# A streamed fp32 encoder layer: where the row work of 32 gathered tokens stands in VectorE's queue, and an expert product with both activation parts in one matmul

## The chip, the cores and the metric

The kernel runs on one core of a Trainium2 chip. The metric is the device time of one execution in microseconds. Engines are named as in the profile: PE (TensorE matmul), PEld (its weight load), DVE (VectorE), ACT (ScalarE), POOL (GpSimd) and SP (SyncE, which here only starts transfers).

## The reference, cut to what matters

One layer over 256 tokens of width 2048 in fp32. The work in question is its last part, a feed-forward layer of 16384 experts of one neuron each, of which each token uses 8 heads times 16:

```python
def block(args):
    xb, eb, gb = args          # tokens, their expert numbers, their gates
    u = expert_u[eb]
    pre = jnp.einsum('bd,bed->be', xb, u)
    act = gelu(pre) * gb
    return jnp.einsum('be,bed->bd', act, expert_v[eb])
```

`expert_u` and `expert_v` are 16384 x 2048 each, 128 MB, and are read from HBM.

## The kernel before, in words

**Two ways through the experts.** The first 224 tokens (`T`) are computed dense: every expert's first product for every token, times a gate that is zero for unused experts, and then every expert's second product. The last 32 tokens (`SP`) take the expert rows that they need: 32 times, POOL starts an indirect DMA (L766) that brings one row of 2048 values to each of the 128 partitions into one of three row buffers, and DVE reduces it against the tokens (L789, which ends in a short readout of the sum); then 32 times a row of `peer_v` that DVE scales and adds up (L802, L804). These 64 instructions are called the rows here.

**The weight stream.** All large operands come as tiles `w` of 128 x 2048 (1 MB) in `wtile`: SP starts the transfer into one of three buffers, ACT casts the tile to a rounded `wh` (L95), DVE subtracts to the rest `wl` (L97); `wh` and `wl` have two buffers each. With `pool=512` POOL does the last 512 of the 2048 columns of `wl` (L99 and L100). The activations are split in the same way, and a product is three products: high by high, low by high, high by low.

**The stages.** `u_steps(q)` for q = 0..3 does the first product, 32 tiles each: per tile 16 pairs of a matmul of 448 columns (`wh` with the high and low half of the tokens side by side, L834) and one of 224 (`wl`, L835), then ACT copies one half of the result (L837), DVE adds the other (L838), ACT applies GELU (L839); the results are the tiles `P0` to `P7` of 16 each. During `u(1)` the steps of `gate_steps` make the dense gates: DVE builds one-hots (L860, L862), PE multiplies them (L877), POOL writes them to `gd` in HBM. `prep_steps(c)` loads the gates of one `P` in two transfers of 0.9 MB into buffers of the same ring as the weights (L910), multiplies (16 instructions, L913) and splits into `ah` and `al` (L104 on ACT, L105 on DVE). `v_steps(q)` does the second product, 32 tiles each: for two values of n, four output blocks `ds` of four tiles `e`; per tile 16 triples of 224 columns (L956 to L958) into four PSUM banks, one for each f. After the fourth tile of a block, DVE adds each bank to `yT` (L964; for n = 0 ACT copies it, L962). The banks come from a pool of four, so a block's bank is the next block's.

**What sets the order.** `run_spread` and `with_last` set in which order the program is written: the rows are spread over the steps of `v(0)`, `u(2)`, `v(1)`, `u(3)`, `v(2)`, `v(3)`, the gate steps over `u(1)`, and `prep` over the last steps of the `u` stages and steps within `v`. A scheduler then places each engine's instructions by readiness on a clock of its own, and each engine runs its list in that order. The context `tc.issue_after(i)` keeps an instruction behind the instruction `i` in that placing. Before, none of the rows has such an edge.

Of the kernel before, what the change touches and what calls it, by code (L numbers as in the profile page):

```python
# [34 lines left out]
def block_kernel(ctx: ExitStack, tc: tile.TileContext, a: dict, out: bass.AP):  # L35
# [735 lines left out]
    def sparse_input():  # L771
        two = [X([P, 2, D], F32, f"rows{i}") for i in range(2)]
        bufs.extend((two[0][:, 1], two[1][:, 0], two[1][:, 1]))
        xs = two[0][:, 0]
# [8 lines left out]
        nc.vector.scalar_tensor_tensor(xs, xs, rs, gb, op0=ALU.mult, op1=ALU.mult)  # L783
        return xs

    def sparse_steps(xs):
# [11 lines left out]
        for k in range(SP):  # L798
            g = rows_of(a["peer_v"], k)
            ak = act[:, k : k + 1]  # L800
            if k == 0:
                nc.vector.tensor_scalar(y, g, ak, None, op0=ALU.mult)  # L802
            else:
                nc.vector.scalar_tensor_tensor(y, g, ak, y, op0=ALU.mult, op1=ALU.add)  # L804
# [96 lines left out]
    def prep_steps(c):  # L901
# [13 lines left out]
        for e in range(4):
            ah = M([P, 4, T], F32R, f"ah{c}_{e}")
            pv = pt[:, 4 * e : 4 * e + 4, :]
            al = M([P, 4, T], F32R, f"al{c}_{e}")
            split(ah, al, pv)
            parts[c, e] = (ah, al)  # L920
            yield
# [157 lines left out]
```

## Time and profile before

| | |
|---|---|
| median of 3 runs | 2864.82 us (2861.01 to 2867.58) |
| the profiled execution | 2864.39 us |
| its span in the trace | 2862.6 us |
| mean granted clock of PE | 0.945 of full speed |
| `u(0)` to the end (from 1094.4 us) | 1768.2 us |

| stage | from | to | us | tiles |
|---|---|---|---|---|
| `u(0)`, `u(1)` | 1094.4 | 1596.4 | 502.0 | 64 |
| `v(0)` | 1596.4 | 1940.4 | 344.0 | 32 |
| `u(2)` | 1940.4 | 2111.0 | 170.6 | 32 |
| `v(1)` | 2111.0 | 2291.7 | 180.7 | 32 |
| `u(3)` | 2291.7 | 2462.2 | 170.5 | 32 |
| `v(2)`, `v(3)` | 2462.2 | 2849.5 | 387.3 | 64 |
| the rest | 2849.5 | 2862.6 | 13.1 | |

The stages are cut at PE's first matmul of each, and tiles are counted from 0 over `u(0)` and `u(1)` (0 to 63), `v(0)` (64 to 95) and so on. A time of this table is where one tile's matmuls begin.

### The profile page before, as it was taken

Reading aid. Unit: us, or ns where it says so; the run is one execution under the profiler, and the core shown is the slowest. Engines: PE = TensorE matmul, PEld = TensorE weight load, DVE = VectorE, ACT = ScalarE, POOL = GpSimd, SP = SyncE. Lnnn points to the kernel's source line nnn. Section 1 sums busy time; section 2 is a strip of 40 time slices with the busy share of each in tenths; the row PEclk is TensorE's granted clock in tenths of the full one; section 3 lists DMA queues with packets and bytes.
Section 4 is the critical chain, followed back from the end, with each engine's and each line's share of the span. In section 5 each row is a group of like instructions: output and inputs, shape, how many; then the busy total and the mean of one; then the engine's idle time right before and its main releaser. Section 6 shows DMA issues by size and latency. Waiting matters only on the chain. (4 is left out here: it accounts for less than half of the span.)

```text
span 2862.6 us, 38540 instructions
## 1 busy us (share of the span) xinstructions
PE 2546.0 (89%) x16314; PEld 2330.4 (81%) x16314; DVE 1648.3 (58%) x1961; ACT 1154.2 (40%) x1314; POOL 305.7 (11%) x216
## 2 busy tenths in 40 slices
PE   8999999999999998696688733499999999999998
PEld 7888888888888887695688633499989998899898
DVE  5655444565554579944776656745555455455554
ACT  5444334454444454342354301134443344333343
POOL 0000000000000001263344225300000000000000
PEclk9999999999999999898799866699999999999999
DMA  6544556545444644375676677755555555755553
GB/s 251 197 171 177 191 191 220 191 177 182 172 165 175 209 174 148 111 254 217 235 230 225 250 273 293 279 203 208 204 205 219 202 206 190 284 190 190 196 184 133
DMA packets 84812, 584.65 MB, mean 204 GB/s; under 512 B 9792, under 2 KB 9856, under 8 KB 18720
## 3 DMA queue, kind: packets, MB, share of 16 engines
q1 hardware_dynamic: 67904, 480.28, 47.2%
q0 software_dynamic: 16592, 101.88, 9.9%
q8 instruction: 128, 2.10, 0.3%
q14 instruction: 44, 0.36, 0.0%
q10 hardware_dynamic: 144, 0.03, 0.0%
HBM read 559.58 MB, written 22.54 MB: 203 GB/s over the span
## 5 line engine op out<-in xcount | busy, mean ns | idle before, releaser
L97 DVE TENSOR_TENSOR wl<-w,wh 128x2048 fp32r<-128x2048 f32 (+2 forms) x400 | 862.6, 2163 | 770.2 <-ACT wh L95 770.0
L95 ACT CAST wh<-w 128x2048 fp32r<-128x2048 f32 (+2 forms) x464 | 841.2, 1818 | 893.8 <-PE v L957 403.5
L958 PE MATMUL v<-ah,wl 128*128 128x224 f32 x2048 | 582.8, 285 | 145.6 <-DVE wl L97 145.6
L834 PE MATMUL u<-a,wh 128*128 128x448 f32 x2048 | 679.8, 388 | 3.4 <-ACT wh L95 3.4
L835 PE MATMUL u<-a,wl 128*128 128x224 f32 x2048 | 558.8, 273 | 74.2 <-DVE wl L100 60.9
L956 PE MATMUL v<-ah,wh 128*128 128x224 f32 x2048 | 582.3, 284 | 24.0 <-ACT yT L962 14.1
L957 PE MATMUL v<-al,wh 128*128 128x224 f32 x2048 | 577.9, 282 | 0.0
L958 PEld LDWEIGHTS v<-ah,wl 128*128 128x128 f32 x2048 | 411.7, 201 | 149.1 <-DVE wl L97 149.1
L835 PEld LDWEIGHTS u<-a,wl 128*128 128x128 f32 x2048 | 408.0, 199 | 81.0 <-DVE wl L100 65.9
L956 PEld LDWEIGHTS v<-ah,wh 128*128 128x128 f32 x2048 | 411.9, 201 | 26.5 <-ACT yT L962 14.5
L834 PEld LDWEIGHTS u<-a,wh 128*128 128x128 f32 x2048 | 401.6, 196 | 35.5 <-ACT wh L95 3.9
L957 PEld LDWEIGHTS v<-al,wh 128*128 128x128 f32 x2048 | 411.3, 201 | 0.5 <-issue 0.5
L839 ACT ACTIVATE P<-P 128x224 f32<-128x224 f32 x128 | 50.1, 391 | 371.0 <-DVE P L838 371.0
L100 POOL TENSOR_TENSOR wl<-w,wh 128x512 fp32r<-128x512 f32 x64 | 138.2, 2160 | 291.2 <-ACT wh L95 225.8
L100 DVE TENSOR_TENSOR wl<-w,wh 128x1536 fp32r<-128x1536 f32 x64 | 114.5, 1790 | 94.6 <-ACT wh L95 94.6
L119 PE MATMUL g<-wh,x 128*128 128x512 f32 x256 | 100.2, 391 | 0.0
L121 PE MATMUL g<-wl,x 128*128 128x512 f32 x256 | 99.6, 389 | 0.0
L120 PE MATMUL g<-wh,x 128*128 128x512 f32 x256 | 99.6, 389 | 0.0
L141 PE MATMUL mq<-hq,wh 128*128 128x512 f32 x256 | 90.8, 399 | 0.0
L141 PE MATMUL pq<-hf,wh 128*128 128x512 f32 x256 | 90.8, 398 | 0.0
L141 PE MATMUL qk<-x,wh 128*128 128x512 f32 x256 | 90.2, 397 | 0.2 <-DVE qk L147 0.2
L141 PE MATMUL mk<-mem,wh 128*128 128x512 f32 x256 | 89.7, 396 | 0.0
(323 smaller groups left out, 3554.9 us busy)
## 6 DMA issues: line engine op xcount, KB each, us to landing
w<-in_peer_uT SPq DMA_DIRECT2D x128, 1024.0 KB, 4.8
w<-in_peer_vP SPq DMA_DIRECT2D x128, 1024.0 KB, 4.8
w<-in_w_in SPq DMA_DIRECT2D x72, 1024.0 KB, 4.8
w<-in_mem_w_kv SPq DMA_DIRECT2D x32, 1024.0 KB, 4.8
w<-in_w_out SPq DMA_DIRECT2D x16, 1024.0 KB, 4.8
w<-in_mem_w_q SPq DMA_DIRECT2D x16, 1024.0 KB, 4.8
w<-in_mem_w_o SPq DMA_DIRECT2D x16, 1024.0 KB, 4.9
w<-in_peer_w_q SPq DMA_DIRECT2D x16, 1024.0 KB, 4.8
```

Source lines behind the costliest of these rows:

```text
L95: nc.scalar.copy(wh[:, c], w[:, c])
L97: nc.vector.tensor_tensor(wl[:, c], w[:, c], wh[:, c].bitcast(F32), op=ALU.subtract)
L100: e.tensor_tensor(wl[:, c], w[:, c], wh[:, c].bitcast(F32), op=ALU.subtract)
L119: nc.tensor.matmul(po[b], xh, wh[:, k, :], start=(kk == 0), stop=False)
L120: nc.tensor.matmul(po[b], xl, wh[:, k, :], start=False, stop=False)
L121: nc.tensor.matmul(po[b], xh, wl[:, k, :], start=False, stop=(kk == nkc * 4 - 1))
L141: nc.tensor.matmul(po[f], wh[:, k, fs], xT.both(kk), start=(kk == 0), stop=False)
L834: nc.tensor.matmul(po[:, 0 : 2 * T], wh[:, k, :], aT.both(k), start=(k == 0), stop=False)
L835: nc.tensor.matmul(po[:, 0:T], wl[:, k, :], aT.tiles[k // 8][:, k % 8, 0], start=False, stop=(k == NK - 1))
L956: nc.tensor.matmul(o, wh[:, j, fs], ah[:, j, :], start=first, stop=False)
L957: nc.tensor.matmul(o, wh[:, j, fs], al[:, j, :], start=False, stop=False)
L958: nc.tensor.matmul(o, wl[:, j, fs], ah[:, j, :], start=False, stop=last)
```

## The change

1. `wtile` notes the last DVE instruction that makes a `wl`. Each row instruction, the product that makes the tokens' input (L783) and the gate products of `prep` are written with `issue_after` that instruction, so that they stand behind the `wl` of the latest tile written.
2. `sparse_input` takes a row buffer for `g_ffn` instead of a weight buffer, and its product is written after `u(1)` instead of before it.
3. `u(1)` no longer gives 512 columns to POOL; the gate steps are spread over 25 tiles instead of 27.
4. `prep`: transfer and products are a step apart, both halves of an activation part stand in one tile `ahl` of two experts' width (8 tiles instead of 4 pairs), and `prep(2)` becomes the first part of the spread stages. It gets 7 last steps of a `u` stage instead of 6. The rows are spread over 174 steps instead of 168.
5. `v_steps`: 16 pairs of 448 and 224 columns per tile in place of 16 triples of 224. The bank's two halves are added to `yT` by two DVE instructions; for n = 0 ACT copies one and DVE adds the other.

```diff
@@ wtile
-                nc.vector.tensor_tensor(wl[:, c], w[:, c], wh[:, c].bitcast(F32), op=ALU.subtract)
+                last_split[0] = nc.vector.tensor_tensor(wl[:, c], w[:, c], wh[:, c].bitcast(F32), op=ALU.subtract).ins
...
@@ sparse_input
-        xs = two[0][:, 0]
+        xs, gb = two[0][:, 0], bufs[2]
...
-        n_w[0] += 1
-        gb = stream.tile([P, D], F32, tag="w", name=f"w{n_w[0]}", bufs=3)
...
-        nc.vector.scalar_tensor_tensor(xs, xs, rs, gb, op0=ALU.mult, op1=ALU.mult)
-        return xs
+        yield
+        with tc.issue_after(last_split[0]):
+            nc.vector.scalar_tensor_tensor(xs, xs, rs, gb, op0=ALU.mult, op1=ALU.mult)
+        yield xs
@@ sparse_steps (the rows of peer_v likewise)
-            nc.vector.tensor_tensor_reduce(
-                g, g, xs, 1.0, 0.0, op0=ALU.mult, op1=ALU.add, accum_out=act[:, k : k + 1]
-            )
+            with tc.issue_after(last_split[0]):
+                nc.vector.tensor_tensor_reduce(
+                    g, g, xs, 1.0, 0.0, op0=ALU.mult, op1=ALU.add, accum_out=act[:, k : k + 1]
+                )
@@ u_steps
-            wh, wl = wtile(a["peer_uT"][j], 512 if q < 2 else 0)
+            wh, wl = wtile(a["peer_uT"][j], 512 if q == 0 else 0)
@@ prep_steps
-        for b in range(2):
-            n_w[0] += 1
-            g = stream.tile([P, T // 16, 8, 16], F32, tag="w", name=f"w{n_w[0]}", bufs=3)
-            nc.sync.dma_start(g, gd[:, 2 * c + b])
-            for j in range(8):
-                pv = pt[:, 8 * b + j, :].rearrange("p (b t) -> p b t", t=16)
-                nc.vector.tensor_tensor(pv, pv, g[:, :, j, :], op=ALU.mult)
+        g = []
+        for b in range(3):
+            if b > 0:
+                with tc.issue_after(last_split[0]):
+                    for j in range(8):
+                        pv = pt[:, 8 * b - 8 + j, :].rearrange("p (b t) -> p b t", t=16)
+                        nc.vector.tensor_tensor(pv, pv, g[b - 1][:, :, j, :], op=ALU.mult)
+            if b < 2:
+                n_w[0] += 1
+                g.append(stream.tile([P, T // 16, 8, 16], F32, tag="w", name=f"w{n_w[0]}", bufs=3))
+                nc.sync.dma_start(g[b], gd[:, 2 * c + b])
             yield
...
+            for i in range(2):
+                ahl = M([P, 2, 2, T], F32R, f"a{c}_{e}{i}")
+                j = 4 * e + 2 * i
+                split(ahl[:, :, 0, :], ahl[:, :, 1, :], pt[:, j : j + 2, :])
+                parts[c, 2 * e + i] = ahl
@@ v_steps
-                            nc.tensor.matmul(o, wh[:, j, fs], ah[:, j, :], start=first, stop=False)
-                            nc.tensor.matmul(o, wh[:, j, fs], al[:, j, :], start=False, stop=False)
-                            nc.tensor.matmul(o, wl[:, j, fs], ah[:, j, :], start=False, stop=last)
+                            ahl = parts[c, 2 * e + j // 2][:, j % 2]
+                            nc.tensor.matmul(
+                                po[f][:, 0 : 2 * T], wh[:, j, fs], ahl.rearrange("p e t -> p (e t)"),
+                                start=first, stop=False,
+                            )
+                            nc.tensor.matmul(po[f][:, 0:T], wl[:, j, fs], ahl[:, 0, :], start=False, stop=last)
...
-                                nc.scalar.copy(y, o)
+                                nc.scalar.copy(y, po[f][:, T : 2 * T])
                             else:
-                                nc.vector.tensor_tensor(y, y, o, op=ALU.add)
-                    if ds == 3 or (ds, e) in ((1, 0), (2, 0)):
+                                nc.vector.tensor_tensor(y, po[f][:, T : 2 * T], y, op=ALU.add)
+                            nc.vector.tensor_tensor(y, po[f][:, 0:T], y, op=ALU.add)
+                    if ds == 3 or (ds, e) in ((1, 0), (1, 3), (2, 2)):
...
@@ the stages
-    xs = sparse_input()
-    run_spread(u_steps(1), 27, gate_steps(), T // TB + 1)
-    run(prep_steps(2))
+    sp = sparse_input()
+    next(sp)
+    run_spread(u_steps(1), 25, gate_steps(), T // TB + 1)
+    xs = next(sp)
     rest = chain(
+        prep_steps(2),
         v_steps(0),
-        with_last(u_steps(2), 6, prep_steps(4)),
+        with_last(u_steps(2), 7, prep_steps(4)),
...
-    run_spread(rest, 168, sparse_steps(xs), 2 * SP + 1)
+    run_spread(rest, 174, sparse_steps(xs), 2 * SP + 1)
```

Three places show what moves. All are lists of DVE, and a line number of the changed kernel is a few higher than that of the same line before (L789 is L794, L97 is L98, L804 is L810, L913 is L919). A row of L789 is two instructions, the second being the readout.

**Place 1, DVE early in `v(0)`.** `wl256` and `wl258` are the rest parts of two weight tiles, `rows` the row buffers. Before:

```order
L97 TENSOR_TENSOR wl256_12163<-w256_12160,wh256_12162 128x2048
L789 ISA rows1_9662,act_8013<-rows1_9662,rows0_9661 128x2048
L789 ISA act_8013 128x1
L789 ISA rows1_9662,act_8013<-rows1_9662,rows0_9661 128x2048
L789 ISA act_8013 128x1
L789 ISA rows1_9662,act_8013<-rows1_9662,rows0_9661 128x2048
L789 ISA act_8013 128x1
L97 TENSOR_TENSOR wl258_12227<-w258_12224,wh258_12226 128x2048
L789 ISA rows1_9662,act_8013<-rows1_9662,rows0_9661 128x2048
L789 ISA act_8013 128x1
L789 ISA rows1_9662,act_8013<-rows1_9662,rows0_9661 128x2048
L789 ISA act_8013 128x1
```

The change, in the same stage:

```order
L98 TENSOR_TENSOR wl253_11994<-w253_11991,wh253_11993 128x2048
L98 TENSOR_TENSOR wl254_12032<-w254_12029,wh254_12031 128x2048
L794 ISA rows0_9661,act_8013<-rows0_9661 128x2048
L794 ISA act_8013 128x1
L98 TENSOR_TENSOR wl255_12084<-w255_12081,wh255_12083 128x2048
L976 TENSOR_TENSOR yT_11908<-v2_0_0_11909,yT_11908 128x224
L976 TENSOR_TENSOR yT_11908<-v2_0_1_11910,yT_11908 128x224
L976 TENSOR_TENSOR yT_11908<-v2_0_2_11911,yT_11908 128x224
L98 TENSOR_TENSOR wl257_12124<-w257_12121,wh257_12123 128x2048
L976 TENSOR_TENSOR yT_11908<-v2_0_3_11912,yT_11908 128x224
L98 TENSOR_TENSOR wl258_12162<-w258_12159,wh258_12161 128x2048
L794 ISA rows1_9662,act_8013<-rows1_9662,rows0_9661 128x2048
```

Before, three rows stand between `wl256` and `wl258` and five between `wl258` and `wl259`; in the change at most one row stands between two `wl`.

**Place 2, DVE at the border of `u(1)` and `v(0)`.** `u62` and `u63` are the last results of `u(1)`, `P3` their tile, and `w257` the gates of half a `prep`. Before:

```order
L97 TENSOR_TENSOR wl252_11937<-w252_11934,wh252_11936 128x2048
L838 TENSOR_TENSOR P3_10850<-u62_11807,P3_10850 128x224
L97 TENSOR_TENSOR wl253_11991<-w253_11988,wh253_11990 128x2048
L838 TENSOR_TENSOR P3_10850<-u63_11850,P3_10850 128x224
L97 TENSOR_TENSOR wl254_12045<-w254_12042,wh254_12044 128x2048
L913 TENSOR_TENSOR P3_10850<-P3_10850,w257_12214 128x224 x8
L97 TENSOR_TENSOR wl255_12101<-w255_12098,wh255_12100 128x2048
L97 TENSOR_TENSOR wl256_12163<-w256_12160,wh256_12162 128x2048
```

The change (`w249` and `w250` are the gates of `prep(2)`, `a2_00` and so on the parts that the first tile of `v(0)` and those after it use, `wl248` belongs to the last tile of `u(1)`, and `wl251` to the first of `v(0)`; five more `a2` parts and one more row follow before `wl251`):

```order
L844 TENSOR_TENSOR P3_10862<-u60_11691,P3_10862 128x224
L98 TENSOR_TENSOR wl248_11821<-w248_11818,wh248_11820 128x2048
L844 TENSOR_TENSOR P3_10862<-u61_11733,P3_10862 128x224
L787 SCALAR_TENSOR_TENSOR rows0_9661<-rows0_9661,rs_9663,rows1_9662 128x2048
L919 TENSOR_TENSOR P2_9673<-P2_9673,w249_11860 128x224 x8
L919 TENSOR_TENSOR P2_9673<-P2_9673,w250_11870 128x224 x8
L794 ISA rows0_9661,act_8013<-rows0_9661 128x2048
L794 ISA act_8013 128x1
L844 TENSOR_TENSOR P3_10862<-u62_11775,P3_10862 128x224
L108 TENSOR_TENSOR a2_00_11882<-P2_9673,a2_00_11882 128x2x224
L108 TENSOR_TENSOR a2_01_11885<-P2_9673,a2_01_11885 128x2x224
L108 TENSOR_TENSOR a2_10_11888<-P2_9673,a2_10_11888 128x2x224
```

All 16 products of `prep(2)`, the tokens' product L787, two rows and the eight parts stand between the last `wl` of `u(1)` and the first of `v(0)`; before, that `prep` stands between the `wl` of three tiles of `u(1)`, and here there is one `P` addition or one group of eight products (those of `prep(3)`) between two `wl`.

**Place 3, DVE where one output block of `v` ends and the next begins** (`v4_0_0` is the bank f = 0 of block 0 of c = 4). Before:

```order
L97 TENSOR_TENSOR wl324_15429<-w324_15426,wh324_15428 128x2048
L964 TENSOR_TENSOR yT_11929<-yT_11929,v4_0_0_15194 128x224
L964 TENSOR_TENSOR yT_11929<-yT_11929,v4_0_1_15195 128x224
L964 TENSOR_TENSOR yT_11929<-yT_11929,v4_0_2_15196 128x224
L964 TENSOR_TENSOR yT_11929<-yT_11929,v4_0_3_15197 128x224
L97 TENSOR_TENSOR wl326_15493<-w326_15490,wh326_15492 128x2048
L97 TENSOR_TENSOR wl327_15549<-w327_15546,wh327_15548 128x2048
```

The change, at such a place with a row:

```order
L98 TENSOR_TENSOR wl341_15596<-w341_15593,wh341_15595 128x2048
L975 TENSOR_TENSOR yT_11908<-v5_0_0_15423,yT_11908 128x224
L810 SCALAR_TENSOR_TENSOR rows0_9661<-rows1_9662,act_8013,rows0_9661 128x2048
L976 TENSOR_TENSOR yT_11908<-v5_0_0_15423,yT_11908 128x224
L975 TENSOR_TENSOR yT_11908<-v5_0_1_15424,yT_11908 128x224
L975 TENSOR_TENSOR yT_11908<-v5_0_2_15425,yT_11908 128x224
L976 TENSOR_TENSOR yT_11908<-v5_0_1_15424,yT_11908 128x224
L976 TENSOR_TENSOR yT_11908<-v5_0_2_15425,yT_11908 128x224
L975 TENSOR_TENSOR yT_11908<-v5_0_3_15426,yT_11908 128x224
L976 TENSOR_TENSOR yT_11908<-v5_0_3_15426,yT_11908 128x224
L98 TENSOR_TENSOR wl342_15636<-w342_15633,wh342_15635 128x2048
```

The four additions behind a `wl` became eight, and at some blocks a row stands between the two additions of one bank. Of the 28 blocks with n above 0, seven have a row among their additions.

## Rows read from the trace of the kernel before

**Rows 1.** The page: its first line and PE's part of the 40 slices of 71.6 us each (busy share and granted clock in tenths).
```profile
span 2862.6 us, 38540 instructions
...
PE   8999999999999998696688733499999999999998
...
PEclk9999999999999999898799866699999999999999
```

**Rows 2.** Busy time by stretch: the stretch, its length, then busy us and count of PE, PEld, DVE, ACT and POOL, the granted clock, the DMA share and GB/s. The stretches are tiles 30 and 31 of `u`, `u(1)`, the 20 tiles of `u(1)` from tile 40 on, `v(0)`, a part of `v(0)`, `u(2)`, `v(1)`, `u(3)` and `v(2)` with `v(3)`.
```profile
1297.90:1322.80 24.90, 15.15 (x70) 13.71 (x68) 10.89 (x9) 4.85 (x6) 6.11 (x3) 0.73 0.56 210
1322.80:1596.40 273.60, 208.71 (x1474) 191.96 (x1473) 191.42 (x220) 116.65 (x213) 109.64 (x72) 0.90 0.67 227
1421.00:1565.00 144.00, 127.27 (x980) 117.27 (x978) 110.33 (x124) 74.84 (x148) 65.95 (x42) 0.98 0.68 225
1596.40:1940.40 344.00, 201.95 (x1538) 199.02 (x1537) 208.37 (x146) 69.99 (x58) 88.39 (x50) 0.77 0.70 261
1629.00:1849.00 220.00, 81.20 (x476) 78.82 (x477) 145.99 (x95) 23.33 (x24) 84.70 (x48) 0.64 0.75 284
1940.40:2111.00 170.60, 163.78 (x1027) 155.41 (x1025) 91.99 (x84) 83.47 (x98) 0.00 (x0) 0.98 0.59 208
2111.00:2291.70 180.70, 174.21 (x1539) 173.50 (x1538) 92.82 (x84) 65.17 (x39) 0.58 (x1) 0.99 0.59 208
2291.70:2462.20 170.50, 164.01 (x1027) 155.60 (x1026) 91.99 (x84) 83.32 (x98) 1.60 (x3) 0.98 0.61 220
2462.20:2849.50 387.30, 364.81 (x3108) 360.13 (x3107) 203.22 (x203) 134.99 (x90) 0.53 (x1) 0.96 0.52 188
```

**Rows 3.** Waits of 1596 to 1861 us: engine, line, releaser: us in total, times, longest.
```profile
PE v L958 <- DVE wl L97: 119.5, 10, 20.2
...
DVE rows L789 <- DMA rows<-in_peer_u,sx: 42.1, 15, 5.8
DVE rows L804 <- DMA rows<-in_peer_v,sx: 34.2, 16, 6.7
```

**Rows 4.** Timeline of 1640 to 1662 us, all engines: start, duration, instruction, idle time of its engine before it and what ended that.
```profile
1648.71 2.29 DVE L789 CUSTOM_DVE_ANT_0 rows<-rows,rows 128x2048 f32<-128x2048 f32 x1 [3.24 <-DMA rows<-in_peer_u,sx]
1650.93 0.08 DVE L789 DVE_READ_ACCUMULATOR2_ANT act<- 128x1 f32 x1
...
1653.61 2.29 DVE L97 TENSOR_TENSOR wl<-w,wh 128x2048 fp32r<-128x2048 f32 x1
...
1655.95 0.55 PE L958 MATMUL v<-ah,wl 128*128 128x224 f32 x1 [10.50 <-DVE wl L97]
```

**Rows 5.** Timeline of ACT, the first two rows in `v(0)`, the last two in `u(2)`: successive casts of weight tiles where nothing waits.
```profile
1892.26 1.91 ACT L95 CAST wh<-w 128x2048 fp32r<-128x2048 f32 x1 [3.45 <-PE v L957]
1897.62 1.91 ACT L95 CAST wh<-w 128x2048 fp32r<-128x2048 f32 x1 [3.45 <-PE v L957]
...
1975.65 1.91 ACT L95 CAST wh<-w 128x2048 fp32r<-128x2048 f32 x1
...
1980.66 1.91 ACT L95 CAST wh<-w 128x2048 fp32r<-128x2048 f32 x1
```

**Rows 6.** Groups of DVE instructions by line and shape, 1596 to 2863 us: line, names, shapes, count | busy us, mean ns | idle before.
```profile
L97 DVE TENSOR_TENSOR wl<-w,wh 128x2048 fp32r<-128x2048 f32 x191 | 436.9, 2291 | 357.9 <-ACT wh L95 357.9
L804 DVE SCALAR_TENSOR_TENSOR rows<-rows,act,rows 128x2048 f32<-128x2048 f32 x21 | 49.4, 2350 | 13.7 <-DMA rows<-in_peer_v,sx 13.3
...
L964 DVE TENSOR_TENSOR yT<-yT,v 128x224 f32<-128x224 f32 x112 | 39.5, 384 | 41.7 <-PE v L958 41.7
L913 DVE TENSOR_TENSOR P<-P,w 128x224 f32<-128x224 f32 x80 | 25.2, 386 | 44.0 <-DMA w<-gd 44.0
...
L105 DVE TENSOR_TENSOR al<-P,ah 128x896 fp32r<-128x896 f32 x20 | 21.6, 1090 | 13.7 <-ACT ah L104 13.6
```

**Rows 7.** Timeline of DVE in `u(2)` where nothing waits.
```profile
1977.59 2.29 DVE L97 TENSOR_TENSOR wl<-w,wh 128x2048 fp32r<-128x2048 f32 x1 [2.42 <-ACT wh L95]
1979.80 0.38 DVE L838 TENSOR_TENSOR P<-u,P 128x224 f32<-128x224 f32 x1
```

**Rows 8.** Timeline of DVE at the border of `u(0)` and `u(1)`.
```profile
1298.30 2.35 DVE L783 SCALAR_TENSOR_TENSOR rows<-rows,rs,w 128x2048 f32<-128x2048 f32 x1 [6.24 <-DMA w<-in_g_ffn]
...
1312.26 2.29 DVE L789 CUSTOM_DVE_ANT_0 rows<-rows 128x2048 f32<-128x2048 f32 x1 [7.30 <-DMA rows<-in_peer_u,sx]
```

**Rows 9.** Busy time of single lines in 1421 to 1565 us, columns PE, PEld, clock, DMA share, GB/s: first the wide `u` matmul (L834, 16 a tile), then the gate matmul (L877, 16 a step).
```profile
1421.00:1565.00 144.00, 104.90 (x320) 60.94 (x321) 0.98 0.68 225
...
1421.00:1565.00 144.00, 26.59 (x340) 21.04 (x337) 0.98 0.68 225
```

**Rows 10.** Timeline of DVE near the end of `u(2)`.
```profile
2065.00 2.50 DVE L913 TENSOR_TENSOR P<-P,w 128x224 f32<-128x224 f32 x8 [4.60 <-DMA w<-gd]
...
2075.87 2.20 DVE L913 TENSOR_TENSOR P<-P,w 128x224 f32<-128x224 f32 x7 [3.86 <-DMA w<-gd]
```

**Rows 11.** DMA issues, 1596 to 2863 us: names, queue, operation, count, KB each, median us from issue to landing.
```profile
w<-gd SPq DMA_DIRECT2D x14, 896.0 KB, 5.4
...
gf<-in_g_final POOLq DMA_DIRECT2D x1, 1024.0 KB, 14.4
rows<-in_peer_v,sx POOLq DMA_INDIRECT x31, 7.8
rows<-in_peer_u,sx POOLq DMA_INDIRECT x19, 7.3
```

More of the change, by code (lines that the diff above doesn't have):

```diff
@@ L83, in block_kernel @@
     n_w = [0]
+    last_split = [None]
     def wtile(src, pool=0, parts=1):
@@ L96, in wtile @@
             if not pool:
-                nc.vector.tensor_tensor(wl[:, c], w[:, c], wh[:, c].bitcast(F32), op=ALU.subtract)
+                last_split[0] = nc.vector.tensor_tensor(wl[:, c], w[:, c], wh[:, c].bitcast(F32), op=ALU.subtract).ins
         if pool:
             for e, c in ((nc.vector, slice(0, D - pool)), (nc.gpsimd, slice(D - pool, D))):
-                e.tensor_tensor(wl[:, c], w[:, c], wh[:, c].bitcast(F32), op=ALU.subtract)
+                i = e.tensor_tensor(wl[:, c], w[:, c], wh[:, c].bitcast(F32), op=ALU.subtract).ins
+                if e is nc.vector:
+                    last_split[0] = i
         return wh, wl
@@ L800, in sparse_steps @@
             ak = act[:, k : k + 1]
[L801 to L804, printed above, removed]
+            with tc.issue_after(last_split[0]):
+                if k == 0:
+                    nc.vector.tensor_scalar(y, g, ak, None, op0=ALU.mult)
+                else:
+                    nc.vector.scalar_tensor_tensor(y, g, ak, y, op0=ALU.mult, op1=ALU.add)
             yield
@@ L906, in prep_steps @@
         pt = ptiles[c]
-        for b in range(2):
-            n_w[0] += 1
-            g = stream.tile([P, T // 16, 8, 16], F32, tag="w", name=f"w{n_w[0]}", bufs=3)
-            nc.sync.dma_start(g, gd[:, 2 * c + b])
-            for j in range(8):
-                pv = pt[:, 8 * b + j, :].rearrange("p (b t) -> p b t", t=16)
-                nc.vector.tensor_tensor(pv, pv, g[:, :, j, :], op=ALU.mult)
+        g = []
+        for b in range(3):
+            if b > 0:
+                with tc.issue_after(last_split[0]):
+                    for j in range(8):
[5 more added lines that the diff above has]
+                nc.sync.dma_start(g[b], gd[:, 2 * c + b])
             yield
         for e in range(4):
[L916 to L920, printed above, removed]
+            for i in range(2):
[3 more added lines that the diff above has]
+                parts[c, 2 * e + i] = ahl
             yield
@@ L998, in block_kernel @@
     run_spread(u_steps(0), 31, chain(side, select_steps(1), select_steps(0)), 4 + 18 + 18)
-    xs = sparse_input()
-    run_spread(u_steps(1), 27, gate_steps(), T // TB + 1)
-    run(prep_steps(2))
+    sp = sparse_input()
+    next(sp)
+    run_spread(u_steps(1), 25, gate_steps(), T // TB + 1)
+    xs = next(sp)
     rest = chain(
+        prep_steps(2),
         v_steps(0),
-        with_last(u_steps(2), 6, prep_steps(4)),
+        with_last(u_steps(2), 7, prep_steps(4)),
         v_steps(1),
-        with_last(u_steps(3), 6, prep_steps(6)),
+        with_last(u_steps(3), 7, prep_steps(6)),
         v_steps(2),
```

2 lines of the change are left out of this document (removed).

## The prediction

> **What bounds the kernel now.** I read the page's slices first. PE is at nine tenths nearly everywhere and falls twice: in slices 18 to 22 (the end of `u(0)` and `u(1)`) and to 3 and 4 in slices 24 to 26, where the granted clock falls too [rows 1]. The stretches say where that is [rows 2]. `v(0)` takes 344.0 us for its 32 tiles; its part from 1629 to 1849 us takes 220 us with PE busy for 81.2 and DVE for 146.0.
>
> The waits of that part [rows 3] put 119.5 us of PE's idle time on `wl` in 10 waits of up to 20.2 us; DVE in turn waited 42.1 and 34.2 us for gathered rows. The timeline shows one such case whole [rows 4]: DVE waits 3.24 us for a gather, does the row (2.29 and a readout of 0.08), does another, and only then makes the `wl` for which PE has stood 10.50 us. Place 1 in the order explains it: five rows in a row ahead of one `wl`. So the bound of this stage is DVE's list: given weight tiles stand behind rows whose gathers (7.3 to 7.8 us each [rows 11]) come later than the list assumed.
>
> Where nothing waits PE bounds. One cast of a weight tile per tile gives the pitch [rows 5]: 1980.66 - 1975.65 = 5.01 us for a `u` tile, 1897.62 - 1892.26 = 5.36 for a `v` tile. Both are 16 times 672 columns; two matmuls (448 and 224) instead of three cost 0.35 us less per tile.
>
> **The gap that a row must fit.** In a `u` tile DVE makes `wl` in 2.29 us, adds in 0.38, and then waits 2.42 for the next cast [rows 7]. With two `wh` buffers a cast begins when PE goes on to the next tile, so PE wants the `wl` of that cast one pitch later: cast at 1975.65 [rows 5], `wl` at 1977.59 + 2.29 = 1979.88, wanted by 1980.66, or some 0.1 earlier for the release of the buffer. So `wl` may come about 0.65 us later. The gap, 2.42 + 0.65 = 3.1 us, holds one row (2.29 + 0.08, or 2.35 [rows 4, 6]), not two. In a `v` tile of the new pitch the 0.38 falls away.
>
> **The change, stage by stage**, against the profiled 2864.4 us (0.4 under the median; 1.8 us of it lie outside the span):
>
> *Tiles 30 and 31.* 24.9 us [rows 2]: L783 waits 6.24 us for `g_ffn`, and a row waits 7.30 for its gather, ahead of `wl` [rows 8]. Both move behind `u(1)`. Two tiles at 5.01: 10.0. **-14.9.**
>
> *`u(1)`.* 273.6 us for 32 tiles and 28 gate steps. In 144.0 us of it there are 320/16 = 20 tiles and 340/16 = 21 steps [rows 2, 9], so a step costs (144.0 - 20 x 5.01)/21 = 2.09 us of PE's time. Left of the rest, 32 x 5.01 + 28 x 2.09 = 218.8. DVE takes over POOL's quarter of `wl`, a quarter of 2.29 [rows 7] or 0.6 us per tile; DVE was busy for 110.3 of the 144.0 us [rows 2], so the spare time hides it and I cost it at nothing; without that cover it is 0.6 x 32 = 18. What is new is the end, place 2: between `wl248` and `wl251` stand L783 (2.35), 16 products (2.50 for eight [rows 10], so 5.0), two rows (4.7), two additions (0.7) and eight parts. A part of 128x2x224 is not in the trace; it lies between 0.38 (128x224) and 1.09 (128x896) [rows 6], I take 0.6, so 4.8. Sum 17.5, less the gap of 3.1: PE stands 14 us, and some 1 us is lost at a lowered clock afterwards. With it 234. Bounds of this end: 6, if the scheduled list runs ahead of PE, and 25, if gates or `g_ffn` (about 14 us, like `gf` [rows 11]) come late too. **-39.6.**
>
> *`v(0)`.* 32 x 5.01 = 160.3. At most one row now stands between two `wl`, and it fits the gap. A gather starts when its buffer was read, three rows back, which is 3 x 2.7 tiles or 40 us; it needs 7.3 to 7.8 [rows 11]. So no row should be waited for. The four block ends of n = 1 have eight additions (0.31 each back to back, from 2.50/8 of the same shape): the first bank's pair of additions comes behind the `wl`, which ends 1979.88 - 1975.65 = 4.2 us after a cast and 4.3 into a tile, and with 2 x 0.38 [rows 6] it ends at 5.1 of 5.01, which costs 0.1 to 0.4. I take 0.4: 162. **-182.** A 448-wide matmul in `v` is not in the trace; its bounds are the pitches 5.01 and 5.36, and I take 5.01 because L834 and L835 stream the same columns from the same kind of tiles.
>
> *`v(1)`.* 180.7. 160.3 + 6 x 0.4 + 2 x 2.4 (place 3, a row between the two additions of the first bank: the next block waits for that bank) = 167.5. **-13.2.**
>
> *`u(2)` and `u(3)`.* 170.6 and 170.5, 10.3 over 32 x 5.01. Two waits for gates, 4.60 and 3.86 us [rows 10], make up most of it; transfer and products a step apart take away most of a landing of 5.4 [rows 11]. But eight products (2.5) and parts in one gap, once with a row, exceed 3.1. Bounds 160.3 and 170.6; I take 168.0 for each. **-5.1.**
>
> *`v(2)` and `v(3)`.* 387.3. 64 x 5.01 = 320.6, 11 x 0.4 + 5 x 2.4 = 16.4 at the block ends, and about 8 for the last column blocks and the `prep` steps among them: 345. Here 387.3 - 64 x 5.36 = 44.3 us were waits, of rows and gates in the list; bounds 325 and 365. **-42.3.**
>
> *The rest.* 13.1 (2862.6 - 2849.5), one addition more per bank: **+0.5.**
>
> Sum -14.9 - 39.6 - 182 - 13.2 - 5.1 - 42.3 + 0.5 = -296.6; 2864.4 - 296.6 = **2568 us**.
>
> **A rule that speaks against one term.** The pitches of [rows 5] give 0.35 us x 128 = 45 us for the wider matmul. The Trainium skill ("TensorE: Matmul & The Clock Gate", section "Back-to-back issue gap") gives for a single matmul N/2.4 + 2.5 ns. By this 448 and 224 columns take 285 ns and three times 224 take 287.5, a difference of 5 us in all instead of 45. The trace disagrees on the sizes, 5.01/16 = 313 ns and 5.36/16 = 335 ns; the same page of the Trainium skill calls the formula one for an isolated matmul, and here they come in a stream.
>
> **Rivals.**
>
> *The `v` pitch stays.* If the 0.35 us belongs to the `u` operands and not to the count of matmuls, the 128 `v` tiles stay at 5.36, +45: 2613. For it: no 448-wide matmul on expert tiles has been seen. Against: the same columns, the same weights per tile, and nothing waits in either stretch. By the Trainium skill's rule above it would be near this, 2568 + 40 = 2608.
>
> *Rows still cost.* If each row makes its `wl` late, say by 2 us since a gap of 3.1 leaves only 0.7, and the next tile cannot win it back: 64 x 2 = 128, so 2696. For it: DVE's list is fuller, and the transfers need 1 MB per 5.01 us and 1 MB per 13.4 (209 + 78 = 287 GB/s), as much as the 284 of the stretch in which gathers were waited for [rows 2]. Against: three buffers give 40 us.
>
> *Gathers starve, on the other side.* Every row's place is now fixed behind a `wl` and ahead of the next; if its gather is late, DVE waits, and the next `wl` with it, 64 times. From 297/64 = 4.6 us per row on, the kernel is slower than before. Such waits are seen: 3.24 us [rows 4], 5.8 and 6.7 at most [rows 3]. At 6 us it would be 2568 + 384 = 2952. But those came where a gather began only one or two rows ahead of its use; with 13.4 us between rows a gather would have to take over 40 us, against 14.4, the longest median [rows 11].
>
> *Nothing but PE is left.* If the border, the block ends and the waits for gates in `prep` all hide: tile 30 begins at 1297.9 [rows 2], and 1297.9 + 10.0 + 218.8 + 6 x 160.3 + 13.1 + 1.8 outside the span is 2503. For it: DVE was busy for only 92 of 170 us in `u(2)` [rows 2]. Against: place 2 lists 17.5 us of DVE work ahead of a `wl` that PE wants at once.
>
> *It doesn't do it.* The edges could leave the rows where they were; place 1 says otherwise.
>
> **How the numbers follow.** Forecast 2568 with a range of its own from 2535 to 2605: 0.60. Pitch stays, 2605 to 2625: 0.13. Between 2503 and 2535: 0.12. Rows still cost, 2625 to 2800: 0.10. Starved gathers, slower than before: 0.03. No effect: 0.02. A range of 2515 to 2640 holds the first two, most of the third and the beginning of the fourth, about 0.82. A measurement of this kernel can't tell a difference under 0.2% (5.7 us) from no change: faster 0.96, same 0.01, slower 0.03.
>
> **What would show it.** Per step: casts in `v` 5.01 us apart; no wait of PE for `wl` over 3 us in `v(0)`, and `v(0)` at 160 to 170 us; one stall of 10 to 20 us where `u(1)` ends; DVE's idle time before rows owed to the gather near zero; stalls of about 2.4 us at seven block ends. It is wrong if DVE shows waits of several us for gathers or if the casts in `v` stand 5.36 apart.

## The result, and the profile after

The changed kernel takes 2616.26 us (median of 4 runs, 2612.45 to 2620.15), 0.913 of the time before (interval 0.9111 to 0.915), 250 us less than the 2866.20 us of the four runs beside it. The profiled execution took 2612.45 us with a span of 2610.7. The forecast was 2568; the range of 2515 to 2640 holds the time, the forecast's own range of 2535 to 2605 does not. Of all runs below one stands apart, a run of e8 that took 10373.59 us: it was not profiled, stays unexplained and is in no interval (e8's 2623.85 us is the median of four with it).

The page's slices, as in [rows 1]:

```profile
span 2610.7 us, 34575 instructions
...
PE   8999999999999999977999988999899999898897
...
PEclk9999999999999999988999989999999999999999
```

The trough of `v(0)` is gone. Two slices at 8 are left where `u(1)` ends (1501 to 1632 us); the two at 7 lie in `u(0)` (1110 to 1240 us), which the change leaves as it was: the 8 and the first 6 of [rows 1] stood there too. The stretches of [rows 2], cut at the same tiles (tiles 30 and 31, `u(1)`, `v(0)`, `u(2)`, `v(1)`, `u(3)`, `v(2)` with `v(3)`; columns as there):

```profile
1300.00:1310.40 10.40, 10.40 (x70) 9.95 (x69) 6.58 (x10) 5.07 (x6) 2.88 (x2) 1.00 0.59 204
1310.40:1524.00 213.60, 194.09 (x1474) 179.57 (x1472) 158.42 (x195) 116.74 (x216) 27.31 (x31) 0.99 0.74 244
1524.00:1704.50 180.50, 165.25 (x1024) 154.78 (x1025) 131.24 (x135) 70.30 (x60) 15.02 (x14) 0.97 0.79 284
1704.50:1875.80 171.30, 164.65 (x1024) 155.72 (x1025) 120.40 (x119) 84.14 (x104) 28.02 (x12) 0.98 0.77 278
1875.80:2054.40 178.60, 166.78 (x1027) 156.66 (x1025) 127.60 (x135) 65.81 (x45) 13.08 (x12) 0.97 0.76 272
2054.40:2220.80 166.40, 162.87 (x1024) 154.58 (x1025) 120.72 (x105) 84.40 (x102) 35.42 (x15) 0.99 0.80 297
2220.80:2597.30 376.50, 343.35 (x2084) 319.97 (x2083) 254.84 (x293) 137.22 (x102) 13.53 (x13) 0.96 0.64 231
```

| stage | before | forecast change | measured change |
|---|---|---|---|
| up to tile 30 | 1297.9 | 0 | +2.1 |
| tiles 30, 31 | 24.9 | -14.9 | -14.5 |
| `u(1)` | 273.6 | -39.6 | -60.0 |
| `v(0)` | 344.0 | -182 | -163.5 |
| `u(2)`, `u(3)` | 341.1 | -5.1 | -3.4 |
| `v(1)` | 180.7 | -13.2 | -2.1 |
| `v(2)`, `v(3)` | 387.3 | -42.3 | -10.8 |
| rest | 13.1 | +0.5 | +0.3 |
| sum | | -296.6 | -251.9 |

The `v` stages brought 61 us less than forecast, 43 of these in `v(1)` to `v(3)`; `u(1)` brought 20 more, and 45 us are missing in all. Groups of DVE's instructions from `v(0)` on, as in [rows 6]: the number after the second bar is the idle time before them.

```profile
L810 DVE SCALAR_TENSOR_TENSOR rows<-rows,act,rows 128x2048 f32<-128x2048 f32 x21 | 49.2, 2344 | 0.0
...
L794 DVE CUSTOM_DVE_ANT_0 rows<-rows,rows 128x2048 f32<-128x2048 f32 x21 | 48.0, 2283 | 0.0
...
L108 DVE TENSOR_TENSOR a<-P,a 128x448 fp32r<-128x448 f32 x47 | 27.5, 620 | 6.4 <-ACT a L107 6.4
```

Not one row waited for its gather any more (42.1 and 34.2 us in [rows 3]); the groups of rows not shown here have 0.0 too. The waits from the end of `u(1)` on, in the columns of [rows 3], name two others:

```profile
ACT wh L96 <- DMA w<-in_peer_vP: 66.2, 14, 9.0
...
PE v L965 <- DVE yT L976: 40.7, 18, 6.2
```

The first of them had no place in the prediction: casts waited 66 us for weights that had not landed. One case whole (timeline of all engines, columns as in [rows 4]):

```profile
2255.29 0.33 SPq L923 DMA_DIRECT2D w<-gd  x1
...
2260.20 2.50 DVE L919 TENSOR_TENSOR P<-P,w 128x224 f32<-128x224 f32 x8
...
2260.32 11.22 SPq L89 DMA_DIRECT2D w<-in_peer_vP  x3
...
2266.96 1.90 ACT L96 CAST wh<-w 128x2048 fp32r<-128x2048 f32 x1 [9.00 <-DMA w<-in_peer_vP]
...
2272.05 0.71 PE L965 MATMUL v<-a,wh 128*128 128x448 f32 x1 [5.92 <-DVE yT L976]
```

The second gate tile of a `prep` starts its transfer at 2255.29 while the first, whose transfer began at 2231.31, still waits for its products (2260.20). Two of the three `w` buffers are then held by gates. The next weight transfer starts only when the last `wl` has freed the third, at 2260.32; ACT gets it at 2266.96, after 9.00 us of waiting, and PE stands 5.92 us: its next block's bank is released by additions that stand behind that tile's `wl`.

### The profile page after: what moved, and what is told of

It reads as the page before. It is cut to its first block, busy times and chain, and to the rows that moved or that the text cites. A ratio compares the mean times of both kernels' runs of the same rounds, so it can differ in the third digit from the quotient of the medians.

```text
span 2610.7 us, 34575 instructions
## 1 busy us (share of the span) xinstructions
PE 2463.8 (94%) x14266; PEld 2214.9 (85%) x14266; DVE 1680.0 (64%) x2121; ACT 1159.7 (44%) x1346; POOL 236.7 (9%) x184
## 3 DMA queue, kind: packets, MB, share of 16 engines
q0 software_dynamic: 16592, 101.88, 10.8%
## 5 line engine op out<-in xcount | busy, mean ns | idle before, releaser
L98 DVE TENSOR_TENSOR wl<-w,wh 128x2048 fp32r<-128x2048 f32 (+2 forms) x432 | 936.6, 2172 | 759.4 <-ACT wh L96 759.0
L965 PE MATMUL v<-a,wh 128*128 128x448 f32 x2048 | 663.8, 383 | 47.3 <-DVE yT L976 40.7
L840 PE MATMUL u<-a,wh 128*128 128x448 f32 x2048 | 666.3, 383 | 4.8 <-ACT wh L96 4.8
L969 PE MATMUL v<-a,wl 128*128 128x224 f32 x2048 | 548.0, 268 | 10.4 <-DVE wl L98 10.4
L965 PEld LDWEIGHTS v<-a,wh 128*128 128x128 f32 x2048 | 392.5, 192 | 85.3 <-ACT wh L96 24.6
L969 PEld LDWEIGHTS v<-a,wl 128*128 128x128 f32 x2048 | 399.1, 195 | 12.6 <-DVE wl L98 11.8
L101 DVE TENSOR_TENSOR wl<-w,wh 128x1536 fp32r<-128x1536 f32 x32 | 57.7, 1802 | 60.6 <-ACT wh L96 60.6
L101 POOL TENSOR_TENSOR wl<-w,wh 128x512 fp32r<-128x512 f32 x32 | 75.9, 2373 | 201.5 <-ACT wh L96 164.2
L769 POOL DMA_INDIRECT rows<-in_peer_v,sx x32 | 54.6, 1706 | 391.9 <-DVE rows L810 327.3
L769 POOL DMA_INDIRECT rows<-in_peer_u,sx x32 | 51.6, 1613 | 374.4 <-DVE act L794 347.5
```

The source lines that it names most:

```text
L98: last_split[0] = nc.vector.tensor_tensor(wl[:, c], w[:, c], wh[:, c].bitcast(F32), op=ALU.subtract).ins
L101: i = e.tensor_tensor(wl[:, c], w[:, c], wh[:, c].bitcast(F32), op=ALU.subtract).ins
L769: nc.gpsimd.indirect_dma_start(g, None, src, bass.IndirectOffsetOnAxis(sx[:, 0, k : k + 1].bitcast(U32), 0))
L840: nc.tensor.matmul(po[:, 0 : 2 * T], wh[:, k, :], aT.both(k), start=(k == 0), stop=False)
L965: nc.tensor.matmul(po[f][:, 0 : 2 * T], wh[:, j, fs], ahl.rearrange("p e t -> p (e t)"), start=first, stop=False,)
L969: nc.tensor.matmul(po[f][:, 0:T], wl[:, j, fs], ahl[:, 0, :], start=False, stop=last)
```

## The experiments

Each stands beside runs of the kernel before on the same chip; intervals are of the ratio to it (the changed kernel: 0.9111 to 0.915). Times of stages and tiles come from one profiled execution each.

**e1, the rows by readiness again, all else as changed.**

```diff
-            with tc.issue_after(last_split[0]):
+            with nullcontext():
... (the same at the rows of peer_v)
```

> The changed kernel with one part undone: the 64 rows again have no edge behind the weight tiles. Theory (the place of the rows in VectorE's list is what the change gained most by): the waits of v(0) come back, v(0) at 300 us or more and the whole at 2760 to 2860 us. Rival (the wider product, the gate tiles and the border are what gained): v(0) stays under 200 us and the whole under 2660.

2718.96 us, 103 more than the changed kernel. `v(0)` in the columns of [rows 2]:

```profile
1523.80:1839.40 315.60, 206.14 (x1025) 186.12 (x1025) 243.13 (x206) 70.85 (x63) 121.70 (x61) 0.80 0.84 319
```

Its waits:

```profile
PE v L969 <- DVE wl L98: 76.4, 17, 9.8
...
DVE rows L794 <- DMA rows<-in_peer_u,sx: 23.9, 10, 4.7
DVE rows L810 <- DMA rows<-in_peer_v,sx: 23.5, 10, 4.5
```

The waits for gathers and for `wl` are back and `v(0)` takes 315.6 instead of 180.5 us, as the theory has it. The whole fell between the two expectations: 135 us are lost in `v(0)`, but 28 won back from `u(2)` on, where no rows are left to do (the last one begins at 1792 us).

**e7, the reverse: the kernel before with only the rows' edges.** The edit is that of the change's `sparse_steps`.

> The kernel before with one part of the change: the 64 rows get the edge behind the latest weight tile. Theory (rows ahead of weight tiles are what v(0) waited for): v(0) from 344 to between 185 and 215 us (its gate products still go by readiness), 2700 to 2745 us. Rival (the rows are only where the lateness shows, and the gates or transfers take their place): over 2780 us.

2672.29 us (0.9318 to 0.9379), 189 less than before with this edit alone, more than expected. `u(1)` and `v(0)`:

```profile
1315.10:1541.60 226.50, 198.76 (x1474) 183.57 (x1473) 166.19 (x195) 116.15 (x212) 98.28 (x60) 0.97 0.69 232
1541.60:1728.40 186.80, 176.21 (x1539) 174.98 (x1538) 113.58 (x93) 69.97 (x55) 17.52 (x14) 0.98 0.72 265
```

Its waits for gates, which this edit leaves:

```profile
DVE P L918 <- DMA w<-gd: 50.1, 12, 10.6
```

`v(0)` is in the expected band with 186.8. What had been left out is `u(1)`, where rows also stood ahead of weight tiles: 226.5 instead of 273.6. The rows' edge is three quarters of the gain by itself; undone in the changed kernel it costs 103, so the other parts without it are worth 147. 189 and 147 are 86 more than the 250 of both: so much is removed by either alone. Which waits these are is not shown.

**e10, the gate products by readiness again.**

```diff
             if b > 0:
-                with tc.issue_after(last_split[0]):
+                with nullcontext():
```

> The changed kernel with the gate products of prep placed by readiness again (no edge behind a weight tile); their steps are as in the change. Theory (the edge gains as it does for the rows, since VectorE waited 4.6 and 3.9 us for gate tiles in the kernel before): waits of VectorE for gates come back, 2630 to 2670 us. Rival (the edge only keeps the gate tile longer in the ring): 2595 to 2618 us.

2643.86 us (0.922 to 0.9265), 28 more, as the theory has it. DVE waits for gates ahead of `wl`, as in [rows 10]:

```profile
DVE P L919 <- DMA w<-gd: 55.6, 11, 10.6
...
PE v L969 <- DVE wl L98: 49.1, 13, 9.3
```

**e2, triples of 224 columns in `v`.**

```diff
-                            nc.tensor.matmul(
-                                po[f][:, 0 : 2 * T], wh[:, j, fs], ahl.rearrange("p e t -> p (e t)"),
-                                start=first, stop=False,
-                            )
+                            nc.tensor.matmul(po[f][:, 0:T], wh[:, j, fs], ahl[:, 0, :], start=first, stop=False)
+                            nc.tensor.matmul(po[f][:, 0:T], wh[:, j, fs], ahl[:, 1, :], start=False, stop=False)
... (and one addition per bank instead of two)
```

> The changed kernel with the output product as 16 triples of 224 columns into one half of the bank, and one addition per bank. Theory (the wider product is worth 0.35 us per tile): casts in v 5.36 us apart, 128 x 0.35 = 45 us more, less some 10 us for the additions that go: 2640 to 2660 us. Rival (by the single-matmul formula only 5 us): 2605 to 2622.

2628.16 us (0.9162 to 0.9208), 12 more, between both expectations. By the starts of the matmuls an undisturbed tile takes 5.36 us here; in the changed kernel the casts in `v` stand 5.01 apart (timeline of ACT, as in [rows 5]):

```profile
1638.45 1.92 ACT L96 CAST wh<-w 128x2048 fp32r<-128x2048 f32 x1 [3.10 <-PE v L965]
1643.46 1.91 ACT L96 CAST wh<-w 128x2048 fp32r<-128x2048 f32 x1 [3.10 <-PE v L965]
```

So the pitch is as forecast, 0.35 x 128 = 45 us; but the `v` tiles' time over their own pitch is 94 us in the changed kernel and 66 here. 28 of the 45 are given back: by the tile starts about 14 at block ends without a row, 11 at the seven with one and 7 at the gates, less 4 at the border.

**e3, gate tiles held for less time.**

```diff
-                    if ds == 3 or (ds, e) in ((1, 0), (1, 3), (2, 2)):
+                    if ds == 3 or (ds, e) in ((1, 0), (1, 1), (1, 2)):
```

> The changed kernel with the first gate tile's products, and the second one's transfer, written after the second tile of the block and not after the fourth (steps at (1,0), (1,1), (1,2)). Theory (a gate tile that keeps its place in the three-buffer ring for four tiles makes the weight transfers start late): the five stalls at the end of the second block, 5 to 8 us each, mostly go, the casts' waits for weight transfers fall from 66 to under 25 us, the whole is at 2580 to 2597 us. Rival (the transfers are slow because the gathers run beside them): 2608 to 2622 us, waits as before.

2603.94 us (0.9073 to 0.9119, which overlaps that of the changed kernel). Neither expectation: the casts' wait fell only from 66 to 45 us, and the stalls moved with the gates instead of going.

```profile
ACT wh L96 <- DMA w<-in_peer_vP: 44.9, 10, 9.2
```

A gate tile within `v` is now held for 17 to 21 us instead of 27 to 34 (from the start of its transfer to its last product), so the time for which one is held was not the whole cause. Two were still there at once, for 7.5 to 11 us in each `prep` within `v`.

**e5, never two gate tiles at once.** Each `prep` has four steps ahead of the parts: transfer, products, transfer, products. In `u(2)` and `u(3)` it gets 8 last steps instead of 7. Within `v` no two gate tiles then stand at once; at the ends of `u(2)` and `u(3)` two still do, for 2.7 us.

```diff
-        for b in range(3):
-            if b > 0:
+        for b in range(2):
...
+            nc.sync.dma_start(g, gd[:, 2 * c + b])
+            yield
+            with tc.issue_after(last_split[0]):
...
-                    if ds == 3 or (ds, e) in ((1, 0), (1, 3), (2, 2)):
+                    if ds == 3 or (ds, e) in ((1, 0), (1, 1), (2, 0), (2, 1)):
...
```

> The changed kernel with the steps of a prep drawn apart: transfer of the first gate tile at (1,0), its products at (1,1), transfer of the second at (2,0), its products at (2,1), so that never two gate tiles are in the ring of three; in u(2) and u(3) 8 steps instead of 7. The rows stand as in the changed kernel. Theory (two gate tiles at once leave one buffer for weights): the stalls of 5 to 8 us in the v stages fall to 2 or less, and some of the 10 and 6 us at the ends of u(2) and u(3) go too, against up to 4 x 2 us where a row now shares a gap with products: 2578 to 2595 us. Rival (one gate tile in the ring costs as much, or the transfers are slowed by the gathers): 2600 to 2620.

2582.01 us (0.9009 to 0.9039), 34 less than the changed kernel, in the theory's band. A gate tile is held as long as in e3 (17 to 22 us), so the 22 us between the two go mainly to two of them standing at once. The casts' wait for weights, and PE's at the banks:

```profile
PE v L963 <- DVE yT L974: 20.9, 14, 2.7
...
ACT wh L96 <- DMA w<-in_peer_vP: 9.9, 3, 3.7
```

**e6, a quarter of the gathers.** 48 of the 64 are left out; DVE's rows stay, on whatever the buffers hold.

```diff
-        nc.gpsimd.indirect_dma_start(
+        if k % 12 < 3:
+            nc.gpsimd.indirect_dma_start(
```

> The changed kernel with 48 of its 64 gathers left out (three of every twelve stay); the rows of VectorE stay, and the results for the 32 tokens are others. Theory (the ring of buffers makes weights late): the stalls at the ends of the second blocks stay over 3 us each, 2598 to 2612 us. Rival (gathers beside the weight transfers make them late): the casts' waits for weight transfers fall under 20 us, and 2575 to 2590 us. If the rows' place itself waited for gathers, more than this would go.

2614.7 us (0.9117 to 0.9148), as the changed kernel; the theory's band ended 3 us lower. The casts still wait 50 us:

```profile
ACT wh L96 <- DMA w<-in_peer_vP: 50.1, 11, 7.3
```

The gathers thus had a part in the casts' wait (50 instead of 66 us), but three quarters of them cost no time that can be measured, and the stalls at the gates stay at 3.9 to 8.3 us. With e5 this settles it: what PE lost to late weights it lost because of the buffers that gates held.

**e4, no row among a block's additions.** `run_spread` starts no row where the tile (`t`, counted from `v(0)` on) is the fourth or first of a block.

```diff
-            while done < due:
+            while done < due and not hold(i):
...
-    run_spread(rest, 174, sparse_steps(xs), 2 * SP + 1)
+    run_spread(rest, 174, sparse_steps(xs), 2 * SP + 1, lambda i: i >= 7 and (lambda t: t // 32 in (0, 2, 4, 5) and t % 4 in (3, 0))(i - 7))
```

> The changed kernel with no row written at the fourth and the first tile of an output block; by the order of VectorE then no row stands among a block's additions. Theory (each of the 7 rows among additions costs 2.3 us of PE's time and 1.7 more at a lowered clock): 7 x (4.0 - 0.9 that a block's end without a row costs) = 21 us less, 2590 to 2602 us. Rival (the row costs as much wherever it stands): 2610 to 2622 us.

2599.97 us (0.9066 to 0.9123; runs 2598.9 to 2609.5), 16 less, in the expected band, though the interval overlaps that of the changed kernel. By the tile starts the seven blocks with a row among the additions ended 2.3 us late in the changed kernel and 0.2 late here.

**e8, `prep(2)` inside the last seven tiles of `u(1)`.**

```diff
-    run_spread(u_steps(1), 25, gate_steps(), T // TB + 1)
+    run_spread(with_last(u_steps(1), 7, prep_steps(2)), 25, gate_steps(), T // TB + 1)
...
```

> The changed kernel with prep(2) in the last seven tiles of u(1) instead of behind them. Theory (17.5 us of VectorE work between two weight tiles stop TensorE for 14 us at the border): that stall goes, and 2 to 4 us come in the last tiles of u(1): 2600 to 2608 us. The rows' places shift by seven tiles, and up to two more stand among additions (8 us). Rival (the products cost TensorE the same wherever they stand): 2613 to 2625.

2623.85 us (0.915 to 0.9186): the theory's gain did not come, and the time is in the rival's band, though for another reason than the rival's. By the tile starts the 14 us at the border went, 16 came in `u(1)`, and the rest of `v(0)` took 10 us more, with three rows among its additions where the changed kernel has none. The stall in `u(1)` (timeline, then SP's wait):

```profile
1484.23 1.77 POOL L898 DMA_DIRECT2D gd<-gs  x2 [7.38 <-ACT gs L893]
...
1488.32 0.33 SPq L923 DMA_DIRECT2D w<-gd  x1
...
1496.01 1.90 ACT L96 CAST wh<-w 128x2048 fp32r<-128x2048 f32 x1 [7.62 <-DMA w<-in_peer_uT]
...
1497.96 0.29 PEld L840 LDWEIGHTS u<-a,wh 128*128 128x128 f32 x1 [11.07 <-ACT wh L96]
1497.96 0.74 PE L840 MATMUL u<-a,wh 128*128 128x448 f32 x1 [10.80 <-ACT wh L96]
...
SPq L923 <- DMA gd<-gs: 30.9, 2, 21.8
```

The last gates go to HBM at 1484.23; the transfer that reads gates back waits in SP's queue for such writes, 21.8 and 9.1 us in a row, and starts at 1488.32. Weight transfers stand behind it in that queue, so PE waits 10.80 us for a cast. In the changed kernel, where the same transfer is written at the border, SP shows no wait for that write.

**e9, GpSimd's share of `wl` in `u(1)` as before** (`512 if q < 2 else 0`).

> The changed kernel with 512 columns of each weight tile's rest part given to GpSimd again in u(1). Theory (VectorE has the time to spare, the part is worth nothing, as the prediction has it): 2610 to 2622 us, u(1) at 213 to 218. Rival (in the kernel before a pair of tiles with gate steps took 13.45 us beside the shared work, 13.17 in the changed kernel without it, so 14 x 0.28 = 4 us, and more where the one-hots run beside GpSimd's part): 2620 to 2635.

2622.25 us (0.9148 to 0.9192), 6 more, just past the theory's band and in the rival's; the interval touches that of the changed kernel. `u(1)` took 219.7 instead of 213.6, where the runs e1 to e6 that keep the whole tile on DVE have 212.2 to 215.3. So giving DVE the whole tile is worth 4 to 7 us in `u(1)`, not nothing.

**e11, what was found, together**: e5's steps, e4's rule (also beside gate products and at the ends of `u(2)` and `u(3)`), one row per tile at most, and the four transfer and product steps of `prep(2)` in the last four tiles of `u(1)`.

> The changed kernel with what the experiments found: the gate tiles drawn apart as in e5, no row at the fourth and first tile of an output block nor beside gate products or the parts at the ends of u(2) and u(3), at most one row per tile, and the transfers and products of prep(2) in the last four tiles of u(1) with its parts behind. Theory (these stalls are each other's neighbours, not each other's cover): e5's 2582 less 16 of e4 and some 8 at the border: 2548 to 2562 us. Rival (what one gives the next takes back): 2570 or more.

2558.07 us (0.8927 to 0.8964; runs 2555.6 to 2559.4), 58 less than the changed kernel, in the theory's band and the fastest here. `v(0)`, and `v(2)` with `v(3)`, then the casts' wait:

```profile
1523.40:1697.50 174.10, 164.60 (x1025) 154.65 (x1025) 127.57 (x131) 71.08 (x62) 16.54 (x13) 0.99 0.79 286
...
2193.70:2544.10 350.40, 338.09 (x2084) 314.49 (x2083) 264.34 (x296) 137.23 (x102) 25.21 (x17) 0.99 0.70 258
...
ACT wh L96 <- DMA w<-in_peer_vP: 40.1, 11, 7.4
```

The casts still wait 40.1 us for weights. That sum alone is therefore no measure of what PE loses: here only one such place, at n = 5, costs it as much as 6 us.

**e12, e11 with triples.**

> e11 with the output product as triples, as in e2. Theory (in the changed kernel the wider product's 45 us were mostly given back, because a shorter tile leaves weights and additions less time; where those stalls are gone, it shows): 30 to 45 us slower than e11. Rival (the wider product is worth 12 us, as e2 against the changed kernel): 8 to 16 us slower than e11.

2574.06 us (0.899 to 0.9031), 16 more than e11: this theory fell, and the rival's band holds it. The same two stages:

```profile
1519.90:1697.20 177.30, 173.58 (x1538) 173.36 (x1537) 118.67 (x103) 71.09 (x61) 16.54 (x13) 0.99 0.77 281
...
2200.80:2557.40 356.60, 352.79 (x3107) 349.14 (x3106) 242.37 (x233) 137.26 (x102) 17.49 (x17) 1.00 0.68 253
```

Over their own pitch the `v` tiles take 48.6 us in e11 (689.9 in all by the tile starts) and 20.3 in e12 (706.3): again 28 of 45 are given back, though most gate stalls are gone. The starts show where: most blocks' ends cost 0.2 to 0.9 us in e11 and nothing in e12, those of n = 7 2.3 against 1.0, those of the first four blocks 0.8 to 2.8 against nothing, and one `prep` (n = 5) 6 us against nothing. Two additions per bank instead of one and a shorter tile would explain the ends; that was read from the tiles and not tried by itself.

## Why the prediction was right or wrong

*What bounds the kernel* was right: rows ahead of weight tiles, each with its gather. e7 and e1 show it from both sides, and in the changed kernel no row waited. The rival of rows that still cost, and that of starved gathers, did not come.

*The number* is in part luck. `u(1)` was too dear by 20 us and the `v` stages too cheap by 61, and these offset each other. The 2616 us also lie in the band of 2605 to 2625 that the prediction gave to the rival of an unchanged pitch, though the pitch did change: the casts in `v` stand 5.01 apart. Of the signs named in advance one failed, `v(0)` at 160 to 170 us: it took 180.5, of which 9 are the border's and the other 11 over its pitch stand at gates and block ends.

*Tiles 30 and 31* were right to 0.4 us.

*`u(1)`* was 20 us too dear. 9 of these are the border's, which fell into the first tile of `v(0)`. The border itself was right: the list of place 2 ran as one block, from the last `wl` of `u(1)` to the next 1529.76 - 1513.44 = 16.3 us (timeline of DVE), and PE lost 14 us (two tiles of 24.0 instead of 10.0).

```profile
1511.15 2.29 DVE L98 TENSOR_TENSOR wl<-w,wh 128x2048 fp32r<-128x2048 f32 x1 [2.42 <-ACT wh L96]
...
1513.66 2.34 DVE L787 SCALAR_TENSOR_TENSOR rows<-rows,rs,rows 128x2048 f32<-128x2048 f32 x1
1515.92 4.92 DVE L919 TENSOR_TENSOR P<-P,w 128x224 f32<-128x224 f32 x16
1520.76 2.29 DVE L794 CUSTOM_DVE_ANT_0 rows<-rows 128x2048 f32<-128x2048 f32 x1
...
1523.27 3.29 DVE L108 TENSOR_TENSOR a<-P,a 128x448 fp32r<-128x448 f32 x6
1526.48 2.29 DVE L794 CUSTOM_DVE_ANT_0 rows<-rows,rows 128x2048 f32<-128x2048 f32 x1
...
1529.76 2.29 DVE L98 TENSOR_TENSOR wl<-w,wh 128x2048 fp32r<-128x2048 f32 x1
```

The rest, some 11 us, is mostly the gate step: (213.6 - 5.0 of the border - 160.3)/28 = 1.73 us instead of 2.09. The prediction costed the removed sharing with GpSimd at nothing; by e9 it is some 6 us. Where the others come from is open. A part of 128x2x224, bounded by 0.38 and 1.09 and taken as 0.6, measured 0.62.

*`v(0)`, `v(1)`, `v(2)` and `v(3)`* were costed at 674.5 us and took 735.6, 61 more, of which 9 are the border's. The step that failed is that of the gates within `v`: "about 8 for the last column blocks and the `prep` steps among them" in the last stages, and nothing in `v(0)` and `v(1)`. The prediction looked at what the gates' products cost on DVE and at the landing of their transfer, and not at the buffers that they take from the weights. That was mis-sized by some 32 us in `v` (e5: its `v` stages take 703.9 instead of 735.6). The 2.4 us for a row between two additions were right (2.3 measured), but after four of the seven came another 1.6 us at a lowered clock, which the sum lacked; e4 took 16 us off. What is left of the 52, some 14, stands mostly at other ends by the tile starts: 1.0 us at each of the four with n = 0, for which the sum had nothing, 0.9 to 1.8 where a `prep`'s parts follow, and 2.3 at those of n = 7. The ordinary ends with n above 0 cost less than the 0.4 of the sum, 0.3.

*The wider matmul*: its pitch was right. The Trainium skill's formula for a single matmul ("TensorE: Matmul & The Clock Gate", section "Back-to-back issue gap"), by which some 5 us would be gained in all (an estimate; the page calls it one for an isolated matmul), is not what these runs show, 5.36 against 5.01 us per tile. That 45 us of pitch bring 12 to 16 of the end time has another cause: 28 are given back, mostly at block ends (e2, e12).

*`u(2)` and `u(3)`*: right within 2 us in sum. In e11, with the gates apart and no row beside them, they take 166.0 and 164.5 us instead of 171.3 and 166.4.

## What to carry to other kernels

Work that waits for data of its own, put by readiness on an engine that also feeds the critical one, goes behind a given piece of feeding work, at most one piece per gap, and with the gap measured first. A tile that borrows a buffer of a streaming ring is costed by the stream's lead that it takes away; here two such tiles at once in a ring of three cost 22 us more than the same tiles, held as long, one after the other (e3, e5). A faster inner loop shortens every gap beside it: look at what the loop's ends must do in the time that is left.

## What was not expected of the hardware

After two stalls of the same length, 2.17 us each, the granted clock differed. The first matmul behind each (timeline of PE):

```profile
2296.32 0.61 PE L965 MATMUL v<-a,wh 128*128 128x448 f32 x1 [2.17 <-DVE yT L976]
...
2341.38 0.44 PE L965 MATMUL v<-a,wh 128*128 128x448 f32 x1 [2.17 <-DVE yT L976]
```

The stretches up to each stall's end and the 2 us from there (the granted clock stands behind the busy times):

```profile
2289.00:2296.20 7.20, 5.15 (x34) 4.67 (x32) 5.18 (x5) 3.81 (x2) 0.06 (x1) 1.00 0.76 279
2296.20:2298.20 2.00, 1.88 (x7) 1.78 (x8) 1.97 (x7) 0.00 (x0) 0.88 (x1) 0.56 0.95 311
...
2334.00:2341.30 7.30, 5.21 (x34) 4.73 (x32) 5.22 (x5) 3.30 (x2) 0.10 (x1) 1.00 0.75 257
2341.30:2343.30 2.00, 1.92 (x12) 1.86 (x13) 1.97 (x7) 0.51 (x1) 0.84 (x1) 1.00 0.91 303
```

After the one it was 0.56 in the mean, near the lower of its two levels (1.2 of 2.4 GHz), and the first matmul took 0.61 us; after the other it was 1.00, and 0.44. Up to both it had been 1.00. What tells them apart no run here shows.
